# Tile addresses moved to multiples of 512 bytes in a two-layer decoder kernel

## The chip, the cores and the metric

The kernel runs on one core of one Trainium2 chip. The metric is the device time of one execution in microseconds; the lower, the better. Three runs of the kernel before took 721.62, 722.7 and 722.75 us, with a median of 722.7 us.

## The reference

The input is x, 256 tokens of width 1024 in fp32, with a memory of 256 rows. Two layers follow each other, and a final RMSNorm ends it. All arithmetic is fp32.

```python
for layer in range(2):
    hn = rmsnorm(h, norm_mix_g[layer])
    if layer == 0:   # 8 stick-breaking heads, 8 softmax heads with rotary q and k, heads of width 64
        h = h + sb_moba_mixer(hn, positions, w_in, w_out)
    else:            # 16 softmax heads with a forget gate for each head
        h = h + fox_mixer(hn, w_in, b_f, w_out)
    h = h + memory_cross_attention(rmsnorm(h, norm_xa_g[layer]), rmsnorm(mem, norm_mem_g[layer]), ...)
    h = h + conv_ffn(rmsnorm(h, norm_ffn_g[layer]), ...)   # 1024 -> 2 x 2816, causal width-3 conv, silu(gate) * val, 2816 -> 1024
return rmsnorm(h, final_norm_g)
```

## The kernel before

Everything is kept with features on the 128 partitions and the 256 tokens along the row. The residual stream h is eight tiles of 128x256. The weights arrive from HBM in blocks of 128x1024 fp32, 512 KB each. `block` (L103) loads one into a `raw` tile and splits it into two parts that add up to it exactly: ScalarE writes `whi`, VectorE writes `wlo`, both in the fp32r type, which TensorE reads in one pass. The activations are split in the same way: `xh`/`xl` for the normed input of a stage, `xn` (L745, in tiles that the q, k, v, mk, mq and mv tags lend) for the normed input of the feedforward, `gh`/`gl` and `part` for the gated features of the feedforward and for attention outputs.

A product is then three products of parts. `proj` (L247) has a 128x128 piece of a weight block stationary and 256 tokens moving:

```python
for k, (xh, xl) in enumerate(xs):
    s = slice(off + k * m, off + k * m + m)
    for w, x in ((b.hi, xh), (b.hi, xl), (b.lo, xh)):
        nc.tensor.matmul(ps[:m], w[:, s], x, start=..., stop=...)
```

so a block of weights is 24 matmuls of 128x128 by 128x256, and each loads new weights into the array. `proj_nat` (L260) has it the other way round, for values: half of an activation tile is stationary and 256 weight columns move. L253 and L267, the matmuls of these two helpers, make 5112 of the kernel's matmuls.

The order of TensorE's work is that of the program text (a manual schedule); the other engines are ordered by the tile framework's scheduler. A row of the profile such as "MATMUL acc<-gh,whi" names the PSUM tile, the moving operand and the stationary one, in this order.

Tiles come from pools, which lie one behind the other in each partition's memory in the order in which they are made: cst, wraw, wsp, act, tmp. In a pool the tiles lie in the order in which they are first asked for, each padded to 32 bytes. The tile `small`, with the norm weights, the conv weights and a few columns, has 426 fp32 numbers a partition (1704 bytes) and lies first, behind 16512 bytes that are reserved. So everything behind it starts off a multiple of 512. Other tiles of 8 bytes a partition (padded to 32) stand between the big ones: `half` (L137) behind `signs`, `rcol` (L231) in the act pool, `ms` (L228), `mx` and `sm` (L384, L385, L668, L669) in the tmp pool. All other sizes are multiples of 512 bytes. What comes out, from the built program, is this: the start of each tile as a remainder by 512.

```
const, signs                              320
masks, sin, cos, mem, raw, whi, wlo,
h, xh, xl                                 352
rrow, gh, gl, part                        416
rt, wide (u, c, xp, xpt, out)             448
diag, q, k, v, s1, s2, pt, sq               0
mk, mq, mv, ct, cs                        192
```

The pieces that TensorE reads of a tile (128 or 256 fp32 columns) start at steps of 512 bytes inside it, but for head slices of 64 columns. So the remainders above are also those of the operands. The eight pairs of `xn` are lent in order: pairs 0 to 4 lie at remainder 0 (q, k, v), pairs 5 to 7 at 192 (mk, mq, mv).

Of the kernel before, what the change touches and what calls it, by code (L numbers as in the profile page):

```python
# [9 lines left out]
F32 = mybir.dt.float32  # L10
# [7 lines left out]
P = 128  # L18
# [16 lines left out]
C_CONV = 72  # L35
C_BF = C_CONV + 2 * 4 * 2 * KF
C_FREQ = C_BF + 1
N_SMALL = C_FREQ + 1

K_ID, K_ONE, K_TRI, K_NONE, K_ROT, K_MASK = 0, 128, 256, 384, 512, 640  # L40
N_CONST = 640 + 128 + 384

# [24 lines left out]
def trunk(ctx: ExitStack, tc: tile.TileContext, a: dict, out: bass.AP):  # L67
    nc = tc.nc

    pool = lambda name, bufs=1, **kw: ctx.enter_context(tc.tile_pool(name=name, bufs=bufs, **kw))  # L70
    cst = pool("cst")
    wraw = pool("wraw", 7)
    wsp = pool("wsp", 5)
    act = pool("act", 1)
    tmp = pool("tmp", 2)
    psA = pool("psA", 2, space=bass.MemoryType.PSUM)
    psS = pool("psS", 4, space=bass.MemoryType.PSUM)
    psO = pool("psO", 1, space=bass.MemoryType.PSUM)
# [3 lines left out]
    def bank(pl, tag, width=512):  # L82
        return pl.tile([P, 512], F32, tag=tag, name=tag)[:, :width]
# [9 lines left out]
                          mybir.DependencyInfo(mybir.DependencyClass.NoSync, mybir.DependencyReason.DATA),  # L93
                          reason="order")

    # ---- weights: one contiguous block per load, split into two exact parts
    fences = []

    # the splits of four blocks, from the one after the next `skip`, come after these two instructions
    def fence(skip, on_act, on_dve):  # L100
        fences.append([skip, on_act, on_dve])

# [15 lines left out]
            f[0] -= 1  # L118
        return Block(hi, lo)

    # ---- inputs and constants
    h2 = [act.tile([P, 2 * T], F32, tag=f"h{k}", name=f"h{k}") for k in range(KD // 2)]
    h = [h2[k // 2][:, (k % 2) * T:(k % 2 + 1) * T] for k in range(KD)]
    small = cst.tile([P, N_SMALL], F32, name="small")
    const = cst.tile([P, N_CONST], F32, name="const")
    raw0 = wraw.tile([P, BLK], F32, tag="raw", name="raw")
    nc.sync.dma_start(small[:, :C_CONV], a["small"][:, :C_CONV])
    for k in range(KD // 2):
        s = slice(k * 2 * P, (k + 1) * 2 * P)
# [4 lines left out]
    tri, negones = signs[:, :P], signs[:, P:]  # L134
    ones = const[:, K_ONE:K_ONE + P]
    rot = const[:, K_ROT:K_ROT + P]
    half = cst.tile([P, 2], F32, name="half")  # L137
    nc.gpsimd.memset(half, -0.5)
    cmask = const[:, K_MASK + P:K_MASK + P + 384]
    masks = cst.tile([P, 2 * P], BF16, name="masks")  # L140
# [1 line left out]

    def late_constants():
        nc.sync.dma_start(const[:, T:], a["const"][:, T:])
        nc.sync.dma_start(small[:, C_CONV:], a["small"][:, C_CONV:])
        nc.vector.tensor_copy(signs, const[:, K_TRI:K_TRI + 2 * P])
        nc.vector.tensor_copy(identb, ident)
        nc.vector.tensor_copy(strict, const[:, K_MASK:K_MASK + P])
# [1 line left out]
    def col(c):  # L150
        return small[:, c:c + 1]

    # ---- exact split of an activation tile
    def split_ps(ps, hi, lo):
        nc.scalar.activation(hi, ps, AF.Copy)
        nc.vector.tensor_sub(lo, ps, hi.bitcast(F32))  # L156
# [29 lines left out]
            split_scaled(h[k], col(G_MIX + k), *res[k])  # L186
        return Block(hi, lo), res

    # the tensor engine's clock rises after some microseconds of work
    def warm_up():  # L190
        w = tmp.tile([P, 512], BF16, tag="rt", name="warm", bufs=2)
        nc.vector.memset(w, 0.0)
        ps = bank(psM, "misc")
        for _ in range(WARM):
            nc.tensor.matmul(ps, w[:, :P], w, start=True, stop=True)

    # ---- reciprocal root mean square over the partitions of eight tiles
    class Stats:
        def __init__(self, keep=""):
            self.n, self.keep = 0, keep  # L200
# [21 lines left out]
        def sums(self, row=True):  # L222
            ps = bank(psM, "misc")
            for t in range(2):
                for i, p in enumerate(self.parts):
                    nc.tensor.matmul(ps[:, 2 * t:2 * t + 1], p[:, t * P:(t + 1) * P], ones[:, 0:1], start=i == 0,  # L226
                                     stop=i == 1)
            ms = tmp.tile([P, 2], F32, tag="ms", name="ms")  # L228
            nc.vector.tensor_scalar(ms, ps[:, 0:4:2], 1.0 / D, EPS, op0=ALU.mult, op1=ALU.add)
            bufs = 1 if self.keep else 2  # L230
            self.col = act.tile([P, 2], F32, tag="rcol" + self.keep, name="rcol", bufs=bufs)  # L231
            nc.gpsimd.tensor_tensor(self.col, ms, half, op=ALU.pow)
            if not row:
                return
            self.dg = tmp.tile([P, T], F32, tag="diag", name="diag", bufs=1)
            for t in range(2):
                nc.vector.tensor_scalar(self.dg[:, t * P:(t + 1) * P], ident, self.col[:, t:t + 1], None, op0=ALU.mult)
# [5 lines left out]
            self.row = act.tile([P, T], F32, tag="rrow" + self.keep, name="rrow", bufs=bufs)  # L243
            nc.scalar.copy(self.row, ps[:, :T])

    # ---- products: weights stationary, tokens moving
    def proj(b, off, xs, ps, first=True, last=True, m=P, hooks={}):  # L247
        n = 0
        for k, (xh, xl) in enumerate(xs):
            s = slice(off + k * m, off + k * m + m)  # L250
            end = last and k == len(xs) - 1
            for w, x in ((b.hi, xh), (b.hi, xl), (b.lo, xh)):
                nc.tensor.matmul(ps[:m], w[:, s], x, start=first and n == 0, stop=end and w is b.lo)  # L253
                n += 1
                if n in hooks:
                    hooks[n]()
        return ps

    # ---- products: tokens stationary, weight columns moving
    def proj_nat(bs, xs, t, ps, hooks={}):  # L260
        s = slice(t * P, (t + 1) * P)
        n = 0
        for k, (xh, xl) in enumerate(xs):
            b = bs[k // 4]
            w = slice((k % 4) * T, (k % 4 + 1) * T)
            for x, y in ((xh, b.hi), (xh, b.lo), (xl, b.hi)):
                nc.tensor.matmul(ps, x[:, s], y[:, w], start=n == 0, stop=n == 3 * KD - 1)  # L267
                n += 1
                if n in hooks:
                    hooks[n]()  # L270
        return ps
# [11 lines left out]
        nc.scalar.activation(x, ps, AF.Copy, scale=st.col[:, t:t + 1])  # L283
        return x

    # ---- scores in two products: both parts of q over both halves of the rows against the high part of k, then the
    # high part of q against the low part of k
    def part():
        return act.tile([P, T], F32R, tag="part", name="part", bufs=NP)

# [20 lines left out]
            res.append(y)  # L311
        return res, lo

    # ---- attention: each step is one visit to the tensor engine with what follows it
    ADD = dict(start=False, stop=True, skip_group_check=True)

    class Stick:
# [37 lines left out]
    class Soft:  # L355
# [25 lines left out]

        def scores(self):
            s, cut = self.s, self.CUT
            mx = tmp.tile([P, 2], F32, tag="mx", name="mx", bufs=3)  # L384
            sm = tmp.tile([P, 2], F32, tag="sm", name="sm", bufs=3)  # L385
            p = self.p = tmp.tile([P, 384], F32, tag="s2", name="s2", bufs=4)
            for i, (c, _, n) in enumerate(cut):
                nc.vector.tensor_tensor_reduce(p[:, c], s[:, c], cmask[:, c], 1.0, -3.0e38, op0=ALU.add, op1=ALU.max,
                                               accum_out=mx[:, i:i + 1])
            nc.vector.tensor_scalar(mx, mx, -1.0, None, op0=ALU.mult)  # L390
            for i, (c, _, _) in enumerate(cut):
                nc.scalar.activation(p[:, c], p[:, c], AF.Exp, bias=mx[:, i:i + 1], accum_out=sm[:, i:i + 1])
            nc.vector.reciprocal(sm, sm)
            for i, (c, _, _) in enumerate(cut):
                nc.vector.tensor_scalar(p[:, c], p[:, c], sm[:, i:i + 1], None, op0=ALU.mult)
# [4 lines left out]
            self.pt = tmp.tile([P, 384], F32, tag="pt", name="pt", bufs=3)  # L400
            nc.scalar.copy(self.pt, self.s)

    # two heads in turn, on the two halves of the array's rows
    def both_products(heads):
        steps = [hd.products() for hd in heads]
        while steps:
# [9 lines left out]
        split_ps(po, *pr)  # L416
        return pr

    # ---- rotary tables
    sin = cst.tile([P, T], F32, name="sin")  # L420
    cos = cst.tile([P, T], F32, name="cos")

# [40 lines left out]
            nc.gpsimd.tensor_tensor(x, x, cos, op=ALU.mult)  # L463
            nc.vector.tensor_add(x, x, t)

    # ---- forget gates: cumulative log decay, exact in three parts
    def decay_rows(ps, st):
        f = lambda n: act.tile([P, T], F32, tag="gh", name=n, bufs=NG)[:16]
        x, e, u, w, one, c = (f(f"f{n}") for n in "xeuw1c")
# [29 lines left out]

        return rows  # L500

    # ---- residual update
    def residual(j, ps, stats):
        nc.vector.tensor_add(h[j], ps, h[j])  # L504
        stats.add(h[j])

    # ---- steps that follow a few products later
    class Pipe:
        def __init__(self):
            self.due = []  # L510
# [141 lines left out]
    class Cross:  # L652
# [12 lines left out]

        def scores(self):
            s = self.s
            mx = tmp.tile([P, 2], F32, tag="mx", name="mx", bufs=3)  # L668
            sm = tmp.tile([P, 2], F32, tag="sm", name="sm", bufs=3)  # L669
            nc.vector.tensor_reduce(mx, s.rearrange("p (t m) -> p t m", t=2), AX.X, ALU.max, negate=True)  # L670
            p = self.p = tmp.tile([P, 512], F32, tag="wide", name="xp", bufs=5)
            cut = [slice(t * T, (t + 1) * T) for t in range(2)]
            for t, c in enumerate(cut):
                nc.scalar.activation(p[:, c], s[:, c], AF.Exp, bias=mx[:, t:t + 1], accum_out=sm[:, t:t + 1])
            nc.vector.reciprocal(sm, sm)
            for t, c in enumerate(cut):
                nc.vector.tensor_scalar(p[:, c], p[:, c], sm[:, t:t + 1], None, op0=ALU.mult)  # L677
# [132 lines left out]
            pending()  # L810
        return nst

    # ---- output: tokens back on the partitions
    fin = []

    def final_tile(j):
# [9 lines left out]

        return turn

    # ---- program
    with tc.manual_schedule(engines={mybir.EngineType.PE}):  # L830
        warm_up()
        st = Stats()
        for layer in range(2):
            st, ms, ks = mixer(layer, st)
# [94 lines left out]
```

## Time and profile before

| | |
|---|---|
| median of three runs | 722.7 us (721.62 to 722.75) |
| profiled execution, span from first to last instruction | 722.0 us |
| mean granted TensorE clock | 0.991 |
| TensorE matmuls busy | 704.6 us, 98% |
| VectorE busy | 576.0 us, 80% |
| ScalarE busy | 467.5 us, 65% |
| HBM read | 114.25 MB, 160 GB/s over the span |

The profiled execution's own time is not listed beside its span; the span alone, 722.0 us, is 0.7 us under the median. TensorE's busy time counts overlapping matmuls as one stretch, and a matmul's length in a row (about 0.28 us) holds its way through the array; what a matmul costs in a dense stream is the distance from its start to the next one's start.

### The profile page before, as it was taken

The page shows a single profiled execution, that of the slowest core. Times are in us where ns is not written, and L with a number is a line of the kernel's source. Part 1 is how long each engine was busy: PE and PEld are TensorE (multiplying, and loading weights), DVE is VectorE, ACT ScalarE, POOL GpSimd, SP SyncE. Part 2 cuts the span into 40 slices and gives each one's busy share as a digit, 9 for nine tenths or more (in the row PEclk, how much of TensorE's full clock was granted, in tenths as well). Part 3 has the DMA queues.
Part 4 walks back from the last instruction along what each step waited for, and adds up shares of the span by engine and source line. Part 5 has one row for each costly group of instructions (what it writes and reads, how often), then busy time and mean ns, then how long its engine had stood idle before and what let it go on. Part 6 is the DMA issues. An engine that isn't in the chain of part 4 may idle for free. (4 is left out here: it accounts for less than half of the span.)

```text
span 722.0 us, 15077 instructions
## 1 busy us (share of the span) xinstructions
PE 704.6 (98%) x5751; PEld 676.4 (94%) x5751; DVE 576.0 (80%) x1195; ACT 467.5 (65%) x942; POOL 74.2 (10%) x82
## 2 busy tenths in 40 slices
PE   8989999999999999999999999999999999999995
PEld 6979998988999999999999889998899999999995
DVE  6997698687999988856569979958889998886541
ACT  6876865567787766644466868646778766664431
POOL 1200020212400000001200000012150000000110
PEclk9989999999999999999999999999999999999998
DMA  8745532343566655665651733516345665556601
GB/s 295 283 144 178 147 118 89 91 147 114 205 191 194 204 195 171 169 182 164 206 172 33 263 120 115 173 43 195 118 176 176 197 211 180 187 167 185 181 9 58
DMA packets 34969, 116.32 MB, mean 161 GB/s; under 512 B 4081, under 2 KB 6225, under 8 KB 34897
## 3 DMA queue, kind: packets, MB, share of 16 engines
q1 hardware_dynamic: 34896, 115.36, 50.5%
q8 instruction: 45, 0.74, 0.4%
q14 instruction: 28, 0.22, 0.1%
HBM read 114.25 MB, written 1.05 MB: 160 GB/s over the span
## 5 line engine op out<-in xcount | busy, mean ns | idle before, releaser
L111 ACT ACTIVATE whi<-raw 128x512 fp32r<-128x512 f32 (+2 forms) x296 | 231.2, 808 | 138.0 <-PE acc L253 85.4
L112 DVE TENSOR_TENSOR wlo<-raw,whi 128x512 fp32r<-128x512 f32 (+2 forms) x296 | 269.6, 927 | 58.9 <-ACT whi L111 56.3
L253 PE MATMUL sc<-xn,whi 128*128 128x256 f32 x768 | 137.7, 281 | 0.0
L253 PEld LDWEIGHTS sc<-xn,whi 128*128 128x128 f32 x768 | 117.8, 188 | 0.0
L253 PE MATMUL acc<-gh,whi 128*128 128x256 f32 x400 | 113.5, 284 | 0.2
L253 PE MATMUL acc<-gl,whi 128*128 128x256 f32 x400 | 111.9, 280 | 0.1
L253 PE MATMUL acc<-gh,wlo 128*128 128x256 f32 x400 | 111.7, 279 | 0.0
L253 PE MATMUL sc<-xn,wlo 128*128 128x256 f32 x384 | 107.7, 281 | 0.0
L253 PE MATMUL acc<-xh,whi 128*128 128x256 f32 x336 | 100.4, 299 | 1.1 <-DVE h L504 0.7
L253 PE MATMUL acc<-xh,wlo 128*128 128x256 f32 x336 | 96.2, 286 | 1.9 <-DVE wlo L112 1.9
L253 PE MATMUL acc<-xl,whi 128*128 128x256 f32 x336 | 97.3, 290 | 0.2
L211 POOL TENSOR_TENSOR sq<-sq 128x256 f32<-128x256 f32 x42 | 41.4, 985 | 513.3 <-ACT sq L205 472.3
L253 PEld LDWEIGHTS acc<-gh,whi 128*128 128x128 f32 x400 | 75.0, 188 | 2.2 <-issue 1.5
L253 PEld LDWEIGHTS acc<-gl,whi 128*128 128x128 f32 x400 | 75.1, 188 | 0.3 <-DVE gl L156 0.3
L253 PEld LDWEIGHTS acc<-gh,wlo 128*128 128x128 f32 x400 | 75.0, 187 | 0.0
L253 PEld LDWEIGHTS sc<-xn,wlo 128*128 128x128 f32 x384 | 72.4, 188 | 0.0
L253 PEld LDWEIGHTS acc<-xh,whi 128*128 128x128 f32 x336 | 65.2, 194 | 5.2 <-issue 2.4
L253 PE MATMUL acc<-xn,whi 128*128 128x256 f32 x384 | 69.3, 281 | 0.0
L253 PEld LDWEIGHTS acc<-xh,wlo 128*128 128x128 f32 x336 | 65.3, 194 | 2.4 <-DVE wlo L112 2.4
L253 PEld LDWEIGHTS acc<-xl,whi 128*128 128x128 f32 x336 | 65.3, 194 | 2.3 <-DVE xl L160 1.6
L253 PEld LDWEIGHTS acc<-xn,whi 128*128 128x128 f32 x384 | 58.9, 188 | 0.0
L253 PE MATMUL acc<-xn,wlo 128*128 128x256 f32 x192 | 53.9, 281 | 0.0
(218 smaller groups left out, 1406.4 us busy)
## 6 DMA issues: line engine op xcount, KB each, us to landing
raw<-up SPq DMA_DIRECT2D x88, 512.0 KB
raw<-down SPq DMA_DIRECT2D x32, 448.0 KB
raw<-fox_in SPq DMA_DIRECT2D x24, 512.0 KB
raw<-ab_in SPq DMA_DIRECT2D x23, 512.0 KB
raw<-down SPq DMA_DIRECT2D x16, 512.0 KB
raw<-ab_out SPq DMA_DIRECT2D x8, 512.0 KB
raw<-fox_out SPq DMA_DIRECT2D x8, 512.0 KB
raw<-xa_k SPq DMA_DIRECT2D x4, 512.0 KB
```

The lines of the kernel that those rows point to most:

```text
L111: i = nc.scalar.activation(hi[:, s], raw[:, s], AF.Copy)
L112: j = nc.vector.tensor_sub(lo[:, s], raw[:, s], hi[:, s].bitcast(F32))
L211: nc.gpsimd.tensor_tensor(sq, sq, self.acc, op=ALU.add)
L253: nc.tensor.matmul(ps[:m], w[:, s], x, start=first and n == 0, stop=end and w is b.lo)
```

## The change

No instruction is added, taken away or moved: on every engine the built program has the same instructions in the same order, and only tile numbers differ. What differs is where tiles lie. `small` is made 472 numbers wide (1888 bytes; the same 426 columns are loaded), `half` is made right behind it, and the two fill the space up to byte 18432. The other 8-byte tiles go into a new pool `tiny`, which is made after `tmp` and so lies behind all the others. By that every remainder in the table above becomes 0: each tile that TensorE reads starts at a multiple of 512 bytes, and all distances between such tiles are multiples of 512 as well.

```diff
+PAD_SMALL = (2048 - 128 - 32) // 4
...
     tmp = pool("tmp", 2)
+    tiny = pool("tiny", 2)
...
-    small = cst.tile([P, N_SMALL], F32, name="small")
+    small = cst.tile([P, PAD_SMALL], F32, name="small")
+    half = cst.tile([P, 2], F32, name="half")
     const = cst.tile([P, N_CONST], F32, name="const")
...
-    half = cst.tile([P, 2], F32, name="half")
     nc.gpsimd.memset(half, -0.5)
...
-        nc.sync.dma_start(small[:, C_CONV:], a["small"][:, C_CONV:])
+        nc.sync.dma_start(small[:, C_CONV:N_SMALL], a["small"][:, C_CONV:])
...
-            ms = tmp.tile([P, 2], F32, tag="ms", name="ms")
+            ms = tiny.tile([P, 2], F32, tag="ms", name="ms")
...
-            self.col = act.tile([P, 2], F32, tag="rcol" + self.keep, name="rcol", bufs=bufs)
+            self.col = tiny.tile([P, 2], F32, tag="rcol" + self.keep, name="rcol", bufs=bufs)
...
-            mx = tmp.tile([P, 2], F32, tag="mx", name="mx", bufs=3)
-            sm = tmp.tile([P, 2], F32, tag="sm", name="sm", bufs=3)
+            mx = tiny.tile([P, 2], F32, tag="mx", name="mx", bufs=3)
+            sm = tiny.tile([P, 2], F32, tag="sm", name="sm", bufs=3)
```

## Rows read from the trace of the kernel before

**Rows 1.** Matmuls of L253 and L267, grouped: busy us, mean ns | idle before.

```profile
L253 PE MATMUL sc<-xn,whi 128*128 128x256 f32 x768 | 137.7, 281 | 0.0
L253 PE MATMUL acc<-gh,whi 128*128 128x256 f32 x400 | 113.5, 284 | 0.2
...
L253 PE MATMUL acc<-xh,whi 128*128 128x256 f32 x336 | 100.4, 299 | 1.1 <-DVE h L504 0.7 <-ACT xh L159 0.4
...
L253 PE MATMUL acc<-xn,whi 128*128 128x256 f32 x384 | 69.3, 281 | 0.0
...
L267 PE MATMUL acc<-whi,xh 128*128 128x256 f32 x120 | 35.4, 295 | 0.3 <-DVE q L276 0.3
L253 PE MATMUL acc<-part,whi 128*128 128x256 f32 x192 | 34.6, 279 | 0.0
...
L253 PE MATMUL sc<-xh,whi 128*128 128x256 f32 x80 | 22.8, 285 | 0.0
...
L253 PE MATMUL sc<-gh,whi 128*128 128x256 f32 x48 | 13.8, 287 | 0.0
...
L267 PE MATMUL acc<-whi,gh 128*128 128x256 f32 x32 | 9.3, 289 | 0.0
```

**Rows 2.** Chain that ended last, second layer: start us, us, what.

```profile
510.74 2.74 PE acc L267 x24
...
535.68 5.76 PE sc L253 x48
...
561.42 5.69 PE sc L253 x48
...
660.50 7.78 PE acc L253 x66
...
707.28 8.23 issue
```

**Rows 3.** Timeline of TensorE, one weight block over xn: start us, us.

```profile
566.95 0.40 PE L253 MATMUL acc<-xn,whi 128*128 128x256 f32 x2
...
568.73 0.40 PE L253 MATMUL acc<-xn,whi 128*128 128x256 f32 x2
...
569.81 0.40 PE L253 MATMUL sc<-xn,whi 128*128 128x256 f32 x2
```

**Rows 4.** Windows: PE, PEld, DVE, ACT, POOL busy us (count), clock, DMA share, GB/s.

```profile
40.70:47.50 6.80, 6.31 (x28) 4.54 (x29) 6.57 (x18) 6.68 (x15) 0.00 (x0) 0.50 0.60 207
47.50:50.00 2.50, 2.50 (x22) 2.50 (x22) 2.50 (x6) 1.32 (x5) 0.00 (x0) 1.00 0.19 34
```

**Rows 5.** Timeline of TensorE, values in layer 0, on both sides of 47.5 us.

```profile
46.23 0.41 PE L267 MATMUL acc<-whi,xl 128*128 128x256 f32 x1
...
47.29 0.39 PE L267 MATMUL acc<-wlo,xh 128*128 128x256 f32 x1
...
47.63 0.28 PE L267 MATMUL acc<-whi,xh 128*128 128x256 f32 x1
...
47.99 0.28 PE L267 MATMUL acc<-whi,xh 128*128 128x256 f32 x1
```

**Rows 6.** Windows of L253, then of L267, first 40 us: PE, PEld, clock, DMA.

```profile
0.00:40.00 40.00, 22.92 (x143) 20.50 (x144) 1.00 0.74 262
...
0.00:40.00 40.00, 6.51 (x48) 6.00 (x48) 1.00 0.74 262
```

**Rows 7.** Timeline of VectorE in the second feedforward: start us, us.

```profile
562.20 0.48 DVE L761 SCALAR_TENSOR_TENSOR c<-acc,small,c 128x254 f32<-128x254 f32 x1
562.59 0.42 DVE L765 TENSOR_TENSOR c<-c 128x256 f32<-128x256 f32 x1
562.93 1.23 DVE L112 TENSOR_TENSOR wlo<-raw,whi 128x1024 fp32r<-128x1024 f32 x1
564.06 0.43 DVE L156 TENSOR_TENSOR part<-c,part 128x256 fp32r<-128x256 f32 x1
```

More of the change, by code (lines that the diff above doesn't have):

```diff
@@ L667, in scores @@
             s = self.s
-            mx = tmp.tile([P, 2], F32, tag="mx", name="mx", bufs=3)
-            sm = tmp.tile([P, 2], F32, tag="sm", name="sm", bufs=3)
+            mx = tiny.tile([P, 2], F32, tag="mx", name="mx", bufs=3)
+            sm = tiny.tile([P, 2], F32, tag="sm", name="sm", bufs=3)
             nc.vector.tensor_reduce(mx, s.rearrange("p (t m) -> p t m", t=2), AX.X, ALU.max, negate=True)
```

## The prediction

> **What bounds the kernel now.** I read the page first: TensorE's matmuls are busy 98% of the span, VectorE 80%, ScalarE 65%. Then the chain that ended last: from some 516 us to 705 us its pieces are matmuls of L253 and little else, one block after the other with no other engine between [rows 2]. So the kernel is bound by how fast TensorE issues its 5112 matmuls of 128x128 by 256 columns. Only a change of that pace, or of the few gaps (the 8.23 us of "issue" at the end is the longest piece that is not a matmul [rows 2]), can change the time.
>
> Next I take the pace from the chain, as length over count, for each kind of moving operand, and set it beside where the operands lie. The stationary operand of `proj` lies at remainder 352 throughout.
>
> - Moving xh and xl (remainder 352): 5.76 us for 48, 120.0 ns [rows 2].
> - Moving gh, gl and part (416): 7.78 us for 66, 117.9 ns [rows 2].
> - Moving xn: 5.69 us for 48, 118.5 ns [rows 2]. Inside a block, the 15 matmuls over pairs 0 to 4 (remainder 0) take from 566.95 to 568.73, 118.7 ns each, and the 9 over pairs 5 to 7 (192) until 569.81, 120.0 ns each [rows 3].
> - Stationary gh and gl (416), moving weights (352), in the cross-attention's values: 2.74 us for 24, 114.2 ns [rows 2].
>
> The same instruction, of the same size and type, thus costs 114.2 to 120.0 ns by the tiles that it reads. What the array itself needs is seen where the clock was low: in 40.7 to 47.5 us the granted clock was 0.50, that is 1.2 GHz [rows 4], and there L267 over xh and whi (352 both) went from 46.23 to 47.29 in five steps, 212 ns each; right behind it, at full clock, three steps took from 47.63 to 47.99, 120 ns each [rows 5]. Half of 212 is 106 ns. So at 2.4 GHz some 8 to 14 ns of every matmul are not the array's pace and not a fixed cost of an instruction, which would show at 1.2 GHz too. They look like operands that come too slowly, and by how much depends on the tiles. This is what the change touches.
>
> A rule speaks against that reading. The Trainium skill ("TensorE: Matmul & The Clock Gate", "Step-by-step: what each phase is for") says that TensorE has two independent read ports, one for the moving operand and one for weight loads, and that loading weights takes no bandwidth from the running matmul; "SBUF — State Buffer" ("Specifications (TRN2)") gives 16-byte lines, on which every tile of this kernel already starts, since all are padded to 32 bytes. By these rules a move of tiles changes nothing and the time stays 722.7 us. The trace does not agree that the address is without effect: it shows 114.2 and 120.0 ns for one and the same form.
>
> **The change, part by part.** Instructions, their order and their waits stay as they are, so there is no new wait and no queue that anything is moved past. The wider `small` costs nothing: the same 426 columns are loaded. The 8-byte tiles in another pool are still 8-byte tiles. What is left is the pace of the 5112 matmuls, once all operands lie at remainder 0.
>
> The trace of before has no full-speed stretch with both operands at 0, so its price is bounded from both sides. Above stands 120.0 ns, the worst row. Below stands 106 ns, the array's own pace by the low clock [rows 5]. I take 114.2 ns, for this reason: with the stationary operand at 352, moving its partner over four remainders shifts the pace by 2 ns at most, while the one stretch whose stationary operand lies elsewhere is 4 to 6 ns faster. It looks as if 352 were a bad place for the stationary operand, and the change takes every one of them from there. That it then meets a place as good as 416 is the choice; the trace doesn't show it.
>
> The sum goes by the counts [rows 1]. A row of "xh,whi" or "gh,whi" is one of three products, a row of "xn,whi" or "part,whi" two of three.
>
> - xh and xl: (336 + 80 + 120) x 3 = 1608 matmuls, from 120.0 to 114.2 ns: 9.3 us.
> - xn: (768 + 384) x 1.5 = 1728, from 118.5: 7.4 us.
> - gh, gl and part moving: (400 + 48) x 3 + 192 x 1.5 = 1632, from 117.9: 6.0 us.
> - gh and gl stationary: 32 x 3 = 96, no change.
>
> That makes 22.7 us. In the first 40 us 143 + 48 of these matmuls run [rows 6], in a stretch where TensorE waits for weights and splits; I give them no gain, 191 x 5.8 ns = 1.1 us. What is late next is VectorE. Per pair of feedforward blocks it has two splits at 1.13 us from start to start, four conv steps at 0.39 and two products of 256 columns at 0.34 [rows 7]: 4.5 us; the first four pairs of a layer have two more products, 5.3 us by 0.39 each. TensorE's 48 matmuls of a pair would take 5.48 us at 114.2 ns. So VectorE still keeps up, barely in the first four, and I take nothing off for it. The weights: 512 KB in 24 x 114.2 ns is 191 GB/s, and the first 40 us moved 262 GB/s [rows 6]. The gain is 21.6 us: the span goes from 722.0 to 700.4, and with the 0.7 us by which the median stands above the profiled span, 701 us.
>
> **The rivals.**
>
> *Slower: equal remainders are the trouble.* The slowest large row, 120.0 ns, is the one whose two operands have the same remainder, 352 and 352 [rows 2]; the fast row has them 64 bytes apart. If two reads that walk in step over equal remainders get in each other's way, the change makes it so everywhere. All then go to 120.0 ns: xn 1728 x 1.5 = 2.6 us, g and part 1632 x 2.1 = 3.4 us, the 96 values 5.8 ns each, 0.6 us; together 6.6 us more, 729.3 us. Against it: 416 with 352 is also 64 bytes apart, the other way round, and takes 117.9, and pairs at 192 with 352 take 120.0 without being equal [rows 2, 3]. It decides from a mean pace above 118.7 ns on. Chance 0.25.
>
> *Much faster: nothing is left of the excess.* At 106 ns the sum is 22.5 + 21.6 + 19.4 + 0.8 = 64.3 us, less 191 x 14 ns = 2.7 us for the first 40 us. A pair would then take TensorE 5.09 us, under VectorE's 5.3 us in the first four of each layer, which gives back 8 x 0.2 = 1.6 us: 60 us less, 663 us. From 112 ns down I count it here (663 to 692 us). For it: the excess is gone at 1.2 GHz [rows 5]. Against it: no full-speed stretch of these matmuls is near it. Chance 0.10.
>
> *A little faster.* The new place is one more of the ordinary ones, like 416 with 352, and only xh and the tail of xn gain: at 117 ns 4.8 + 2.6 + 1.5 = 8.9 us, 714 us. Chance 0.15.
>
> *The change doesn't do what it says.* The pace depends on something that goes along with the tiles (fp32r parts in another order, the other engines' writes), and not on the address: 722.7 us. For it: every comparison above is also one between stages. Against it: inside one block of xn the pace changes from 118.7 to 120.0 at the pair where the remainder does [rows 3]. The skill's two read ports come out here. Chance 0.10.
>
> **How the numbers follow.** The forecast (a pace of 112 to 115.5 ns, 692 to 707 us) has 0.40 and is the likeliest: 701 us. Faster by over 0.2% (1.4 us, about what a measurement of this kernel can tell from no change) is the forecast, the much faster and the little faster: 0.65. Within 0.2%: 0.10. Slower: 0.25. The range of 685 to 730 us holds the forecast, the little faster, no change and the slower case, and leaves out the greater part of the much faster one.
>
> **What the changed profile would show.** Right: in the chain, blocks of 48 over xh, xn and g with one and the same pace, near 5.5 us, whichever tile moves; the stretch of 24 at the cross-attention's values unchanged near 2.74 us; VectorE's rows as long as before, and its share of the span a little higher; few new waits for wlo. Wrong: blocks of 48 near 5.76 us everywhere (equal remainders), or three different paces as before (not the address). If the blocks are faster but the time is not, waits of TensorE for VectorE's splits (L112) must have come in, most likely in the first four pairs of a feedforward.

## The result and the profile after

The changed kernel takes 729.94 us (median of six runs, 727.62 to 730.57), and the kernel before takes 722.73 us in six runs beside it. The ratio is 1.0084, with a 95% interval of 1.0058 to 1.011: it is slower by 0.8%. I had forecast 701 us. The time is within 1 us of the first rival's 729.3 us.

The page of the changed kernel. Lines of the code have moved by three, so L256 is the matmul of `proj` and L270 that of `proj_nat`.

```profile
span 728.3 us, 15077 instructions
...
PE 710.7 (98%) x5751; PEld 683.7 (94%) x5751; DVE 576.3 (79%) x1195; ACT 466.6 (64%) x942; POOL 74.3 (10%) x82
...
L256 PE MATMUL sc<-xn,whi 128*128 128x256 f32 x768 | 139.4, 283 | 0.0
...
L256 PE MATMUL acc<-gh,whi 128*128 128x256 f32 x400 | 115.0, 287 | 0.0
```

No counts have changed, and VectorE and ScalarE work as long as before. TensorE's busy time has grown by 6.1 us, and its rows over xn and gh by 2 to 3 ns a matmul [rows 1].

The chain that ended last, in the same places as [rows 2]:

```profile
514.79 2.87 PE acc L270 x24
...
565.76 5.76 PE sc L256 x48
...
655.04 10.80 PE acc L256 x90
...
666.05 7.92 PE acc L256 x66
...
713.59 8.38 issue
```

Length over count gives the pace: 5.76 us for 48 over xn, 10.80 for 90 and 7.92 for 66 over gh and gl are 120.0 ns each, and 2.87 for 24 in the values is 119.6. Where before there were four paces, 114.2 to 120.0 ns, there is now one, and it is the slowest of them. From the values to the last long wait it is 198.80 us, against 196.54 before [rows 2].

Over all dense stretches at full clock the mean time from one matmul's start to the next's is 118.6 ns before and 119.9 ns after. The difference of 1.3 ns times 5112 matmuls is 6.6 us; the spans differ by 6.3 us and the medians by 7.2. In counts, a window in the first feedforward for L256 (PE and PEld busy us with their counts, clock, DMA share, GB/s):

```profile
220.00:260.00 40.00, 40.00 (x335) 40.00 (x335) 1.00 0.62 198
```

The same window of the kernel before, for L253:

```profile
220.00:260.00 40.00, 40.00 (x340) 40.00 (x339) 1.00 0.64 200
```

In 40 us at full clock, with TensorE never idle, 335 matmuls are issued now and 340 before.

The start of the span needs a caution. There the first 40 us hold fewer matmuls of L256 than in [rows 6], at a mean granted clock of 0.83, against 1.00:

```profile
0.00:40.00 40.00, 22.34 (x129) 19.93 (x130) 0.83 0.73 261
```

Most profiled executions have a stretch at a granted clock of 0.50 in the first 50 us, 3.4 to 13.7 us long in all of them (13.65 us in this one, and about 6.8 us in that of before [rows 4]). It differs between executions of one kernel: of the two profiled executions of `w64` below, one has none and the other has 3.4 us. The times of the kernel before lie between 720.9 and 726.6 us, the longer ones mostly at a lower mean granted clock (721.95 us at 0.997, 726.59 us at 0.987). So a single time below can be off by some us; its paces, taken at full clock, tell more.

### The profile page after: what moved, and what is told of

Its sections match the earlier page's. It is cut to its first block, busy times and chain, and to the rows that moved or that the text cites. A ratio compares the mean times of both kernels' runs of the same rounds, so it can differ in the third digit from the quotient of the medians.

```text
span 728.3 us, 15077 instructions
## 1 busy us (share of the span) xinstructions
PE 710.7 (98%) x5751; PEld 683.7 (94%) x5751; DVE 576.3 (79%) x1195; ACT 466.6 (64%) x942; POOL 74.3 (10%) x82
## 5 line engine op out<-in xcount | busy, mean ns | idle before, releaser
L256 PE MATMUL sc<-xn,whi 128*128 128x256 f32 x768 | 139.4, 283 | 0.0
L256 PEld LDWEIGHTS sc<-xn,whi 128*128 128x128 f32 x768 | 119.8, 192 | 0.0
L256 PE MATMUL acc<-gh,whi 128*128 128x256 f32 x400 | 115.0, 287 | 0.0
L256 PE MATMUL acc<-gl,whi 128*128 128x256 f32 x400 | 113.3, 283 | 0.1
L256 PE MATMUL acc<-gh,wlo 128*128 128x256 f32 x400 | 113.1, 283 | 0.0
L256 PE MATMUL sc<-xn,wlo 128*128 128x256 f32 x384 | 108.7, 283 | 0.0
L256 PE MATMUL acc<-xh,whi 128*128 128x256 f32 x336 | 100.8, 300 | 2.0 <-ACT xh L162 1.2
L256 PE MATMUL acc<-xh,wlo 128*128 128x256 f32 x336 | 96.9, 288 | 1.8 <-DVE wlo L115 1.8
L256 PE MATMUL acc<-xl,whi 128*128 128x256 f32 x336 | 97.8, 291 | 0.3
L256 PEld LDWEIGHTS acc<-gh,whi 128*128 128x128 f32 x400 | 76.6, 192 | 1.8 <-ACT gh L158 0.8
L256 PEld LDWEIGHTS acc<-gl,whi 128*128 128x128 f32 x400 | 76.7, 192 | 0.3 <-DVE gl L159 0.3
L256 PEld LDWEIGHTS acc<-gh,wlo 128*128 128x128 f32 x400 | 76.7, 192 | 0.0
L256 PEld LDWEIGHTS sc<-xn,wlo 128*128 128x128 f32 x384 | 73.7, 192 | 0.0
L256 PEld LDWEIGHTS acc<-xh,whi 128*128 128x128 f32 x336 | 65.8, 196 | 6.1 <-ACT xh L162 2.6
L256 PE MATMUL acc<-xn,whi 128*128 128x256 f32 x384 | 70.2, 283 | 0.0
L256 PEld LDWEIGHTS acc<-xh,wlo 128*128 128x128 f32 x336 | 65.8, 196 | 2.3 <-DVE wlo L115 2.3
L256 PEld LDWEIGHTS acc<-xl,whi 128*128 128x128 f32 x336 | 65.8, 196 | 2.2 <-DVE xl L163 1.6
L256 PEld LDWEIGHTS acc<-xn,whi 128*128 128x128 f32 x384 | 59.9, 192 | 0.0
L256 PE MATMUL acc<-xn,wlo 128*128 128x256 f32 x192 | 54.3, 283 | 0.0
```

## The experiments

A distance below is the start of the stationary operand less that of the moving one, modulo 512 bytes. Before, it is 0 for xh, 352 and 160 for xn, 448 (that is, the moving operand starts 64 bytes further on) for gh, gl and part, and 64 for the values. After, it is 0 everywhere. "Pace" is the mean time from one start to the next in dense stretches at full clock.

**Each half of the change alone.** `pad_only` widens `small` and leaves the 8-byte tiles where they were: all places shift by 160 bytes, and every distance stays as before.

```diff
-    small = cst.tile([P, N_SMALL], F32, name="small")
+    small = cst.tile([P, PAD_SMALL], F32, name="small")
+    half = cst.tile([P, 2], F32, name="half")
```

> One half of the change alone: small is widened and half moved, but ms, rcol, mx and sm stay where they were between the big tiles. Weights and xh/xl then lie at remainder 0, gh/gl/part at 64, the q, k, v tiles of xn at 160, the mk, mq, mv tiles at 352. Every tile is moved by the same 160 bytes (mod 512), so all distances between operands are those of the kernel before. If the distance between the two operands (mod 512) decides the pace: the three paces of before come back (120.0 ns for xh, 117.9 for g and part, 118.5 for xn, 114 for the cross-attention's values) and the time is that of before, 722.7 us, within 0.3%. If the place itself decides (0 is bad for the stationary operand): 120.0 ns everywhere but the 96 values, as in the changed kernel, about 729 us.

`tiny_only` moves the 8-byte tiles behind the others and leaves `small` as it was: all distances become 0, but every tile lies at remainder 352 and none at a multiple of 512.

```diff
+    tiny = pool("tiny", 2)
-            ms = tmp.tile([P, 2], F32, tag="ms", name="ms")
+            ms = tiny.tile([P, 2], F32, tag="ms", name="ms")
```

> The other half alone: the small tiles move behind the others, but small keeps its 426 columns, so every tile that TensorE reads lies at remainder 352, none at a multiple of 512, and all distances are multiples of 512. If the distance decides: 120.0 ns everywhere, as in the changed kernel, 728 to 731 us. If it is the multiple of 512 that hurts: not slower than before, 720 to 724 us.

`pad_only` took 723.09 us, ratio 0.9991 (0.9968 to 1.0014): no change. `tiny_only` took 728.07 us, ratio 1.007 (1.0048 to 1.0091): the loss of the whole change. Their chains, over xn and then over gh and gl, first `pad_only`:

```profile
593.19 5.69 PE sc L255 x48
...
658.11 7.78 PE acc L255 x66
```

and `tiny_only`:

```profile
589.38 5.76 PE sc L256 x48
...
663.76 7.92 PE acc L256 x66
```

`pad_only` has the two paces of before [rows 2], 118.5 and 117.9 ns, though its stationary operand has left remainder 352 for 0. `tiny_only` has 120.0 ns, though its stationary operand is still at 352. So it isn't the place of the stationary operand; what counts is the distance between the two operands, and 0 is as bad as any that this kernel had. One number of `pad_only` came out otherwise than expected: its 96 values take 115.9 ns, against 113.9 before, at the same distance of 64. That distance has more than one pace, as is seen below.

**The weights 64 bytes further on than the activations.** `w64` is the changed kernel with `whi` and `wlo` at remainder 64, and all else at 0.

```diff
     wraw = pool("wraw", 7)
+    pad("pad0", 64)
     wsp = pool("wsp", 5)
+    pad("pad1", 448)
```

> The changed kernel with whi and wlo alone shifted by 64 bytes (64 bytes of padding ahead of their pool, 448 behind it); all other operands stay at 0. If the distance decides, by stationary less moving: in proj it is +64, that of the fast values of the kernel before (stationary 416, moving 352), so 114 ns for all but the L267 matmuls, which get -64 and 118 ns: 5112 x 120 less 4632 x 6 ns is about 27 us under the changed kernel, 701 to 705 us. If the place decides: no forecast from the rows for 64, but the L267 matmuls, whose stationary stays at 0, keep 120 ns. If the values of before were fast for another reason (their stage): 117 to 120 ns, 718 to 730 us.

It took 710.64 us (median of four, 704.98 to 717.25), faster than both kernels; the ratio, taken without the longest of the four, is 0.9795 (0.9739 to 0.985). Only the profiled execution, 704.98 us, lies in the 701 to 705 us expected. In it the pace of `proj` is 114.2 ns, and the values, at 448 now, take 117.1. The chain of `w64`, and TensorE's only wait from 530 to 566 us:

```profile
523.11 5.44 PE sc L262 x48
...
531.27 5.45 PE sc L262 x48
536.73 0.42 DVE c L774
...
555.93 5.70 PE sc L262 x48
...
642.77 7.78 PE acc L262 x66
...
650.76 7.50 PE acc L262 x66
...
PE sc L262 <- ACT c L773: 0.2, 1, 0.2
```

Two things are to be seen. From 536.73 to 555.93 us the chain runs over VectorE: at 5.44 us for 48 matmuls TensorE comes level with it in the first pairs of the second feedforward, as the prediction had it for 114 ns. That costs next to nothing, one wait of 0.2 us, for a step of ScalarE (L773) at the end of that chain. And rows of the same form now take either 7.50 us for 66 or 7.78, 113.6 or 117.9 ns, at one and the same distance.

**Is the cost one of single instructions?** `whi64` puts only `whi` at 64. `wlo`, in a pool of its own, stays at 0, so that of each three matmuls two have the distance 64 and one has 0.

```diff
-        lo = wsp.tile([P, BLK], F32R, tag="wlo", name="wlo")
+        lo = wlp.tile([P, BLK], F32R, tag="wlo", name="wlo")
```

> The changed kernel with whi alone at remainder 64; wlo and all else at 0. It tells which two reads meet. The three matmuls of a triple are (xh, whi), (xl, whi), (xh, wlo). If the moving read meets the weight load of the matmul that follows: from the first to the second start the distance is 64 (114 ns), from the second to the third it is 0, wlo being loaded (120 ns), from the third to the next first it is 64 (114 ns). If what counts is a matmul's own pair of operands: 114, 114, 120 ns. If the distance sets the pace only over a longer run of equal distances: three equal paces between 114 and 120. One run, 708 to 716 us by the first two.

One run of 719.73 us. Its chain, over xn and over gh and gl:

```profile
566.61 5.65 PE sc L262 x48
...
656.57 7.77 PE acc L262 x66
```

In `proj` all three take 117.5 to 118.0 ns, whether 64 or 0 apart; two at 113.3 and one at 120.0 would have made 115.5 on the mean. This is the expectation's last case, three equal paces. So a matmul's pace isn't settled by its own two operands alone: it hangs on those around it too. In the values, where the weights are the moving operand, the three differ: 121.8 ns from the start of a matmul over `wlo` to the next, 116.9 and 117.6 from those over `whi`.

**More distances.** `w320` and `w448` are `w64` with 320 and 448 for the weights.

```diff
-    pad("pad0", 64)
+    pad("pad0", 320)
```

> whi and wlo both at 320, all other operands at 0. In the scan the part tiles had this distance (stationary less moving 320) and 114.6 ns, as good as 64. If the distance sets the pace by itself: 114 to 115 ns for all of proj and 702 to 712 us. If the pace also hangs on what runs before (mq had distance 64 in the scan and still 119.2 ns): anything from 113 to 118 ns, and 702 to 722 us.

> whi and wlo at 448, all other operands at 0: the mirror of the shift by 64 bytes. If only the size of the shift counted, proj would have 114 ns as at 64. If the sign counts too, as the kernel before says (stationary 352, moving 416: 117.9 ns): 117 to 118 ns for proj, 114 ns for the L267 matmuls, whose distance is then +64; 715 to 722 us in one run.

`w320` took 712.73 us (median of four), ratio 0.9835 (0.9761 to 0.9909), with `proj` at 115.6 ns; that is outside the first case expected, 114 to 115 ns for all of `proj`, and inside the second, since the paces of 113.3 and 117.8 ns stand side by side. `w448` took 717.38 us in one run, with `proj` at 117.6 ns and the values at 114.7, as expected if the sign counts. Lines of the chain, two of `w320` and then one of `w448`:

```profile
569.98 5.44 PE sc L262 x48
...
656.14 7.78 PE acc L262 x66
...
564.27 5.65 PE sc L262 x48
```

`scan1` leaves the weights at 0 and gives each kind of activation a pool and a remainder of its own: xh 32, gh 128, part 192, q and k 256, v 320, mk 384, mq 448, mv 480. `scan2` does the same with xn at 192, gh 224, part 288, xh 416.

```diff
+    pad("pad_g", 32)
+    p_g = pool("p_g", 2)
+    pad("pad_part", 64)
+    p_part = pool("p_part", 2)
```

> A scan of distances in one profile: weights stay at 0, and the other operands get a remainder each: xh/xl 32, gh/gl 128, part 192, the q and k tiles 256, v 320, mk 384, mq 448, mv 480. If the distance decides, each kind of moving operand has a pace of its own: mq (stationary less moving +64) 114 ns, the others unknown between 109 and 120; the L267 matmuls over xh show the distance with the other sign. If the place of the stationary operand decides: 120 ns for all of proj, since the weights stay at 0.

> Second scan: weights at 0, all tiles of xn at 192 (distance 320), gh/gl at 224 (288), part at 288 (224), xh/xl at 416 (96). If the distance sets the pace: xn 114 to 115 ns over its whole block, the others unknown between 109 and 120; L267 over xh gets distance 416, over the memory's values 224. If the pace hangs on the tile or the stage and not on the distance: xn keeps 118 to 120 ns.

They took 720.46 and 719.22 us, in one run each. Their paces stand in the table below, beside the next experiment's; xn in `scan2` came out at 115.6 ns, above the 114 to 115 expected.

**The matmuls by themselves.** `alone` leaves out the whole computation: two tiles of weights and two of activations are loaded, and then only TensorE works, in stretches of 48 matmuls in the order of `proj`, each at another distance, up from 0 to 496 by 16 and down again.

```diff
+    for _ in range(blocks):
+        for k in range(8):
+            for iw, ix in ((0, 0), (0, 1), (1, 0)):
+                nc.tensor.matmul(bank[:m, :n], w[iw][:, wo:wo + m], xs[ix][:, xo:xo + n], ...)
+    for d in range(0, 512, 16):
+        stretch(d)
```

> The disputed cost by itself: this kernel leaves out the whole computation (its output is a copy of part of x) and runs stretches of 48 matmuls of the form of proj (two fp32r parts of the weights, two of the tokens, 128x128 stationary, 256 columns moving) from tiles that are written once before; ScalarE, VectorE and DMA are idle meanwhile. Distances (stationary less moving, mod 512) go from 0 to 496 in steps of 16 and back down, then 0, 64, 320, 448 with the moving operand at 352, then 16-column weights, 128 and 512 moving columns at 0, 64, 320. If the distance of TensorE's own two reads makes the pace: 120 ns at 0, 113 to 114 at 64 and 320, 117 to 118 at 448, as in the whole kernel, with all other engines idle. If the other engines' reads and writes make it: about 109 ns at every distance. If what ran before counts as well: the way up and the way down differ at the same distance. If the weight load's length counts: 16-column weights go down to 109 ns at 0; if only its start counts, they stay near 113 to 120.

Windows of `alone` of 5 us each, inside the stretches at 0, 64, 128, 192 and 256, and, on the way down, at 448 (PE, PEld, DVE, ACT, POOL, then clock, DMA share and GB/s):

```profile
19.93:24.93 5.00, 5.00 (x44) 5.00 (x44) 0.00 (x0) 0.00 (x0) 0.00 (x0) 1.00 0.00 0
...
42.70:47.70 5.00, 5.00 (x46) 5.00 (x46) 0.00 (x0) 0.00 (x0) 0.00 (x0) 1.00 0.00 0
65.30:70.30 5.00, 5.00 (x44) 5.00 (x44) 0.00 (x0) 0.00 (x0) 0.00 (x0) 1.00 0.00 0
88.18:93.18 5.00, 5.00 (x46) 5.00 (x46) 0.00 (x0) 0.00 (x0) 0.00 (x0) 1.00 0.00 0
110.58:115.58 5.00, 5.00 (x44) 5.00 (x44) 0.00 (x0) 0.00 (x0) 0.00 (x0) 1.00 0.00 0
...
218.18:223.18 5.00, 5.00 (x44) 5.00 (x44) 0.00 (x0) 0.00 (x0) 0.00 (x0) 1.00 0.00 0
```

Nothing else is running, and the pace still goes by the distance. The paces in ns, by the distance modulo 256 (in `alone` a distance and the one 256 above it differ by 0.2 ns at most on the way up):

```
distance   kernels                                                   alone, up   alone, down
0          119.9 (after), 119.9 (tiny_only), 119.6 (xh before)       120.0       120.0
32         118.3 (scan2, gh)                                         118.4       118.4
64         114.2 (w64), 115.6 (w320), 115.6 (scan2, xn), 114.6       113.4       113.7
           (scan1, part), 113.9 (values before)
96         118.0 (xn before, pairs 0 to 4), 118.0 (scan2, xh)        118.7       118.7
128        118.7 (scan1, gh)                                         118.6       118.5
160        119.7 (xn before, pairs 5 to 7)                           120.0       119.8
192        117.8 (gh, gl, part before), 117.6 (w448)                 113.3       117.8
224        117.0 (scan1, xh), 117.1 (scan2, part)                    116.7       116.8
```

Every row of the kernel before finds its place in this table, within 0.7 ns of one of the two columns of `alone` (which differ by more than 0.3 ns at 192 alone). What doesn't are the operands of `scan1` that change their distance every few matmuls within a block: q and k at 256 (distance 0) came out at 117.8 ns, not 120, and mq at 448 (distance 64) at 119.2, not 114. That is the lesson of `whi64` once more.

The distance isn't all of it even here: with the moving operand at 352 in place of 0, the distances 64 and 320 took 116.7 ns and 448 took 117.3.

`alone` also took 16 weight columns in place of 128, which made 116.7 ns at distance 0 and 117.8 at 64. So the width of the weight load is worth 3.3 ns at distance 0 and nothing at 64; it isn't what makes most of the difference.

**What picks one of the two paces.** At 64 and 192 both 113.3 and 117.8 ns occur. `alone2`, with the computation left out as in `alone`, holds the distance at 64 and then at 0 and goes through 16 places; then it puts 64 and 192 behind stretches of other distances and behind two transposes.

```diff
+    for place in range(0, 512, 32):
+        stretch(place + 64, place)
+    for place in range(0, 512, 32):
+        stretch(place, place)
```

> Again the cost by itself, with the whole computation left out (the output is a copy of part of x). First the place: distance 64 with the moving operand at 0, 32, ... 480 (stationary 64 bytes further), then distance 0 at the same 16 places. If only the distance counts: 113.4 ns at all 16, then 120 ns at all 16. If the place counts too: the 113.4 shows at some places and 116 to 118 at others; 352 gave 116.7 in the stretch before. Then what ran before: stretches of 64 and of 192 right behind a stretch of 0, 48, 112, 144, 160, 208 or 240. If a stretch keeps a state that it starts in: 192 is 113.4 ns behind some and 117.8 behind others; 64 always 113.4 (as in both directions of the scan) or the same two values. Last, 64 and 192 four times each behind two transposes, as in the output's end: if an interruption can put 64 into the slower state, some of the four are near 118.

Its first four stretches at distance 64, then one at distance 0:

```profile
21.27:26.27 5.00, 5.00 (x44) 5.00 (x44) 0.00 (x0) 0.00 (x0) 0.00 (x0) 1.00 0.00 0
26.92:31.92 5.00, 5.00 (x46) 5.00 (x46) 0.00 (x0) 0.00 (x0) 0.00 (x0) 1.00 0.00 0
32.39:37.39 5.00, 5.00 (x44) 5.00 (x44) 0.00 (x0) 0.00 (x0) 0.00 (x0) 1.00 0.01 3
38.04:43.04 5.00, 5.00 (x46) 5.00 (x46) 0.00 (x0) 0.00 (x0) 0.00 (x0) 1.00 0.00 0
...
115.99:120.99 5.00, 5.00 (x44) 5.00 (x44) 0.00 (x0) 0.00 (x0) 0.00 (x0) 1.00 0.00 0
```

At distance 64 the stretches alternate, 117.8, 113.3, 117.8, 113.3 ns, all sixteen, and each keeps its pace to the end. At distance 0 all sixteen have 120.0 ns, wherever they lie. Behind other stretches 64 and 192 come out at either pace: 64 takes 117.8 behind a stretch at 0 and 113.3 behind the six others, and 192 takes 113.3 behind 0, 48, 160 and 208 and 117.8 behind 112, 144 and 240. Distance 64 behind 0, then behind 48:

```profile
208.01:213.01 5.00, 5.00 (x45) 5.00 (x44) 0.00 (x0) 0.00 (x0) 0.00 (x0) 1.00 0.00 0
230.52:235.52 5.00, 5.00 (x47) 5.00 (x46) 0.00 (x0) 0.00 (x0) 0.00 (x0) 1.00 0.00 0
```

The alternation goes with the place modulo 64, and with the PSUM tile, of which four take turns. Neither settles the pace: the seven stretches at 64 behind others have the same place and, by the order of the program, the same PSUM tile, and one of them is slow. So these distances have more than one steady pace, and the start of a stretch picks one. Four stretches at 64, each behind two transposes, took 117.8, 113.3, 113.3 and 117.8 ns; four at 192 took 117.8 each. Other distances have two paces as well: 144 took 116.7 and 120.0 ns, and 240 took 117.4 here and 119.9 in `alone`.

**The better version again, and 192.** `w64_again` is `w64` unchanged. `w192` has the weights at 192, the one of the four distances 64, 192, 320 and 448 not yet tried in the kernel.

```diff
-    pad("pad0", 64)
+    pad("pad0", 192)
```

> The same kernel as w64, for a narrower interval, beside the one with 192. Theory (which of the two paces a stretch takes is set by the order of the instructions, which is fixed): 708 to 712 us, a ratio of 0.977 to 0.987 to the kernel before. Rival (it is set anew in each execution): times spread evenly from 704 to 718 us from one execution to the next.

> The changed kernel with the two weight halves at remainder 192, so that the stationary operand of the projections lies 192 bytes (modulo 512) behind the moving one, and the reduction of the normalisation has -192. Theory (only the distance modulo 256 counts, and distances of 64 and 192 have two paces, 113.3 and 117.8 ns, of which a stretch keeps one): projections between 113.3 and 117.8 ns on the mean, the reduction too, and 704 to 718 us. Rival (64 is a better distance than 192 in itself): projections at 117.8 ns throughout and 716 to 719 us. Rival (alignment counts, not distance): 730 us, as the changed kernel.

`w64_again` took 713.26 us (708.93 to 719.49 in six runs), ratio 0.9869 (0.9829 to 0.9909); `w192` took 720.4 us, ratio 0.9947 (0.992 to 0.9975). Both are slower than their first theories had it. The profiled execution of `w192`, 717.83 us, has `proj` at 117.6 ns:

```profile
564.70 5.65 PE sc L262 x48
```

That agrees with its rival "64 is a better distance than 192 in itself". Taken in groups of 24 matmuls of `proj`, 6 of 191 are at the faster pace in `w192` and 7 of 191 in `w448`, against 161 of 192 in `w64`, 74 of 192 in `w64_again` and 102 of 192 in `w320`. In these kernels, then, 192 (modulo 256) nearly always takes the slower pace, though it can take the faster one in `alone2`. The twelve times of `w192`, 713.5 to 724.41 us, spread more widely than one pace would have it, and only one of the twelve was profiled: what the longer ones ran at isn't shown. (What the expectation calls a reduction are the values of `proj_nat`; they took 115.3 ns.)

For `w64` the first theory fails: the order of the instructions is the same in both, and the paces aren't. Windows of L262 in the first and the second feedforward, first `w64`, with `proj` at 114.2 ns over the whole run:

```profile
190.00:215.00 25.00, 25.00 (x223) 25.00 (x222) 1.00 0.60 173
220.00:355.00 135.00, 135.00 (x1194) 134.77 (x1193) 1.00 0.65 196
560.00:640.00 80.00, 80.00 (x708) 80.00 (x707) 1.00 0.65 198
```

and `w64_again`, the same code, at 116.2 ns:

```profile
190.00:215.00 25.00, 25.00 (x223) 25.00 (x222) 1.00 0.56 171
220.00:355.00 135.00, 135.00 (x1148) 135.00 (x1148) 1.00 0.63 189
560.00:640.00 80.00, 79.81 (x678) 79.64 (x678) 1.00 0.64 194
```

Until 215 us the two executions go alike. From 220 us on one issues a matmul every 113.3 ns and the other every 117.8, for some 135 us without a break. (A window also counts the matmuls that run over its edges.) Between the two lies the only wait of TensorE in that feedforward, which both have:

```profile
217.63 0.48 PE L262 MATMUL sc<-xn,whi 128*128 128x256 f32 x2 [0.16 <-ACT c L773]
```

is that place in `w64`, and in `w64_again` it is

```profile
217.99 0.47 PE L262 MATMUL sc<-xn,whi 128*128 128x256 f32 x2 [0.17 <-ACT c L773]
```

The starts around it are 437 ns apart in the one and 447 in the other. In the second feedforward the same wait stands at 555.9 and 561.7 us, and behind it the two run at 113.3 and 117.8 ns again. What this costs can be read from how far `w64_again` is behind at the same matmul: 0.36 us at the first wait and 5.67 us where that stretch ends, 5.73 us at the second wait and 9.09 us where that one ends. The two stretches, 50 and 32 groups of 24 matmuls, make 5.3 + 3.4 = 8.7 us; the spans (712.0 and 703.2) differ by 8.8. Of the other 111 groups 85 differ by less than half of the 4.5 ns between the two paces, and all that lies outside the two stretches comes to 0.2 us on balance. That each execution picks anew is thus shown by two executions; whether the times spread evenly, as the rival has it, ten can't tell.

## Why the prediction was wrong

**What bounds the kernel** was read rightly. The pace of the matmuls is the kernel's time: a pace higher by 1.3 ns made it longer by about the product with 5112, and the other engines worked as long as before.

**The address has an effect.** This was right, and what the prediction drew from the rule that spoke against it, that a move of tiles changes nothing, is not borne out. The Trainium skill ("TensorE: Matmul & The Clock Gate", "Step-by-step: what each phase is for") has two independent read ports for the moving operand and for weight loads. In `alone`, where TensorE alone is at work, one and the same pair of instructions takes 113.3 to 120.0 ns as its two operands lie. So the trace disagrees with the rule as far as it would have the two operands independent of each other, by up to 6.7 ns a matmul; the reads themselves are seen in no run. Nor is the address all of the 8 to 14 ns that the prediction laid to the operands: the best pace at any distance is still 7 ns above its 106, and that a fixed cost would have to show at the low clock too is not borne out by any run.

**The step that failed** is the price at remainder 0: "I take 114.2 ns ... It looks as if 352 were a bad place for the stationary operand". The measured pace is 120.0 ns. I read the four paces as those of places, since the fast row was the only one whose stationary operand lay elsewhere. They are paces of distances. The fast row differed from the others in that too: it had the distance 64, where the others had 0, 448, 352 and 160. `pad_only` moved the stationary operand from 352 to 0 and left its paces in `proj` as they were; `tiny_only` left it at 352 and made all of them 120.0. The sum then has the wrong sign: in place of 1608 x 5.8 + 1728 x 4.3 + 1632 x 3.7 ns gained, it is 0 for xh, 1728 x 1.5 and 1632 x 2.1 ns lost for xn and for gh, gl and part, and 5.8 ns for each of the 96 values. A small term was off too: the 0.7 us added to the span. In every execution on record that has both, the time is 1.8 us above the span.

**The rival "equal remainders are the trouble"** had the rule and the price for this kernel: 120.0 ns everywhere, 729.3 us. Its reason, two reads that get in each other's way, is not shown. That the stated range still reaches the measured time is owed to this rival, which set its upper end, and not to the forecast. The evidence against it in the prediction was sound but no contradiction: 160 costs 120.0 in its own right, and 448 is not 64 with the sign turned round, for in these kernels it takes 117.8 almost throughout. The rows of before could not tell place from distance, since the fast row differed from the others in both; 0.25 was too little for the one of two readings that explained the fastest and the slowest row by one cause.

**"Much faster"** did not come true at any distance: the best mean pace of a stretch of this form was 113.3 ns, so no layout tried here comes near the 106 ns worked out from the half clock. **"Doesn't do what it says"** is out, by `tiny_only` alone.

**VectorE as the next bound** was right where it could be seen: in `w64`, at 5.44 us a pair, the chain goes over VectorE in the first pairs, and the loss is 0.2 us. The wait matters more by what comes behind it: there the two executions of `w64` part.

Left open is the mechanism. The paces repeat every 256 bytes, depend on neighbouring instructions and stay steady once taken, which looks like two streams of reads that lock into a rhythm; no run here shows the reads themselves. Nor is it shown what in the start of a stretch picks the pace: a wait that differs by 10 ns is all that was seen to go before it. A kernel that restarts TensorE until it gets the faster pace was not tried.

## What to carry to other kernels

Measure a dense matmul stream by the time from start to start, one kind of operands at a time, and set it beside the distance between the stationary and the moving operand, not beside the place of either. Aligning all tiles alike puts every pair at distance 0, which was among the worst here (120.0 ns, in every stretch of this form that held it); an offset of 64 bytes between the pool of weights and that of activations took 1.5% off the time before over all ten executions (median 711.86 us against 723.02). Where the fastest row differs from the others in two ways, the rows can't say which one counts, and a kernel that changes only one of them can.

## What the runs showed of the hardware that was not expected

- With no other engine at work, a 128x128 by 256 matmul in fp32r with new weights takes 113.3 to some 120 ns at full clock, by the distance of its operands modulo 256 bytes.
- At 64 and 192 the same stream has two steady paces, 113.3 and 117.8 ns (and 116.7 at 64 in one place of `alone`). One of them is picked at a restart and kept, in `w64` for over 1,100 matmuls. The ten executions of that kernel took 704.98 to 719.49 us, a spread of 14.5 us where the kernel before has 5.7; for the two profiled ones the picked pace accounts for 8.7 of the 8.8 us between them.
- With 512 columns the order turns round: 226.6 ns at distance 0, once the stretch has settled, and 233.4 at 64 and 320. With 128 columns it is 111.6 ns at all three, little less than with 256. Each was one stretch of 48 matmuls in `alone`.
